# A delta-rule scan with the state's share of u taken from one matrix, formed ahead of the scan and summed in PSUM

## The chip, the cores and the metric

The kernel runs on one core of one Trainium2 chip. The metric is the device time of one execution in microseconds (us); less is better. Engines are named as in the profile: PE is TensorE's matmul (PEld its weight load), DVE is VectorE, ACT is ScalarE, POOL is GpSimd, SP is SyncE, which issues most DMAs.

## What is computed

One decoder layer for 1024 tokens and a width of 1024: a modulated RMSNorm gives h, one large projection of h feeds three token mixers (stick-breaking attention, gated DeltaNet, GLA) and their gates, and the mixers' outputs are projected, weighted, summed and projected once more. The change touches the gated DeltaNet alone. Its core in the reference, per head and per chunk:

```python
u_base, w_kc = sol[..., :dv], sol[..., dv:]
def step(state, inp):
    u_b, w_c, qk_c, qd, kd, cd = inp
    u = u_b - jnp.einsum('bhck,bhkv->bhcv', w_c, state)
    o = jnp.einsum('bhck,bhkv->bhcv', qd, state) + jnp.einsum('bhij,bhjv->bhiv', qk_c, u)
    state = state * cd[..., None, None] + jnp.einsum('bhck,bhcv->bhkv', kd, u)
    return state, o
```

`sol` solves a unit lower-triangular system for each chunk. The kernel has 4 heads and takes chunks of 128 tokens, so 8 chunks a head, in two halves of 4.

## The kernel before

**Order of the work.** PE's order is written out by the program itself; the other engines' instructions are ordered by the framework's scheduler. `emit` (L264) holds a list of tasks, each a generator that yields the time until it wants to go on, counted on a clock that adds up a fixed cost for each matmul. While no task is due, `emit` takes the next piece of the filler: `dense` (L251), the large projections. A piece is six matmuls of 512 columns into an `acc` bank (`run_cm`, L200). So PE's stream is dense work, cut by short bursts of a task. A `yield` of up to about 1300 becomes one piece of six dense matmuls.

**The DeltaNet tasks.** For each of the 8 halves (head h, half q) there are four tasks:

- `gdn_prep` (G.a, L553) transposes k into PSUM (`k_ps`), forms `Kd` (k times its decay, L585), the scalars per row (`rb`, `rn`, L593 to L596), and the triangular matrix A (L603). Then it inverts 16x16 blocks on DVE in 30 small steps (L623, L625) and sends them through DRAM.
- `gdn_inv` (G.b, L635) joins the blocks in four stages of small matmuls to Z, the transposed inverse. It starts a fixed lag after its predecessors. L649 masks the blocks on POOL; L730 writes the last quarter of Z.
- `gdn_vq` (G.v, L733) transposes v and forms `Vb` (L751), forms `qd` on POOL (L773) and `QK` (L779).
- `gdn_scan` (G.s, L781) goes through the four chunks.

**The scan of a chunk**, with S the state (128x128): a first burst computes k^T S into a bank (`s_ps`) and qd S into the output bank `o_ps`. DVE makes R = rn * (k^T S) + Vb (L797). A second burst computes Z R into `u_ps`. DVE copies it to `u` (L804). A third burst computes Kd u into `d_ps` and QK u into `o_ps`. DVE makes the new state Sn = cd * S + d_ps (L813; in a head's first chunk, which has no S, a copy, L811). Between the bursts stand the yields of 500, 1000 and 1200:

```python
s_ps = bank(pm, "mx", P)
mm(s_ps, kT[:, ts], S, 218, start=True, stop=True)
R = mid("r0", P)
nc.vector.scalar_tensor_tensor(out=R, in0=s_ps, scalar=m["rn"][:, i:i + 1],
                               in1=Vb[:, ts], op0=ALU.mult, op1=ALU.add)
mm(o_ps[:, i, :], qd[:, ts], S, 218, start=True, stop=False)
yield 500
u_ps = bank(pm, "mx", P)
mm(u_ps, Z[:, ts], R, 218, start=True, stop=True)
```

`s_ps`, `u_ps` and `d_ps` are separate tiles of the pool `pm`. All these matmuls are fp32, and each stands in the trace as two MATMUL instructions (two passes).

Of the kernel before, what the change touches and what calls it, by code (L numbers as in the profile page):

```python
# [19 lines left out]
P = 128  # L20
# [32 lines left out]
def kernel(ctx: ExitStack, tc: tile.TileContext, xT: bass.AP, c: bass.AP,  # L53
# [19 lines left out]
    def big(tag, w=1024, dt=F32):  # L73
        return mp.tile([P, w], dt, tag=tag, name=tag, bufs=3 if tag == "u5" else 2)

    def mid(tag, w=512, dt=F32):
        return sp.tile([P, w], dt, tag=tag, name=tag, bufs=1 if tag in ONE_MID else 3 if tag in ("c0", "c8", "c9") else 2)
# [225 lines left out]
    def v3(ap, c=4):  # L303
        return ap.rearrange("p (c t) -> p c t", c=c)

    def colb(ap, n, w):
        return ap.unsqueeze(2).broadcast_to([P, n, w])
# [245 lines left out]
    def gdn_prep(st, q):  # L553
        h = st["h"]
        hs = slice(q * HALF, (q + 1) * HALF)
        cs = slice(4 * q, 4 * q + 4)
        qT, kT, vT = (t[:, hs] for t in st["qkv"])
        m = st[q] = {}
        if q == 0:
            st["A"] = big("u7")  # L560
        A = st["A"][:, hs]
        gb = mid("v5")
        nc.sync.dma_start(out=gb, in_=gam_d[h:h + 1, hs].broadcast_to([P, HALF]))
        gl = v3(gb)[:, :, P - 1]
        cd = m["cd"] = mid("c0", 4)
        nc.scalar.activation(out=cd, in_=gl, func=AF.Exp)
        kdc = mid("c1", 4)
        nc.vector.tensor_sub(out=kdc, in0=gl, in1=gam_c[:, cs, h])
        nc.scalar.activation(out=kdc, in_=kdc, func=AF.Exp)
        Kd = m["Kd"] = big("u5")[:, 0:HALF]  # L570
        ss = mid("c2", 4)
        nc.gpsimd.memset(ss, 0.0)
        rr = mid("c3", 4)
        rb = m["rb"] = mid("c8", 4)
        rn = m["rn"] = mid("c9", 4)
        sq = mid("v0")
        yield from tr_free()
        tr_hold(2500)
        k_ps = bank(pt, "tr", 4, P)
        for i in range(4):  # L580
            pe_t(k_ps[:, i, :], kT[:, i * P:(i + 1) * P])
        for i in range(4):
            nc.scalar.activation(out=sq[:, i * P:(i + 1) * P], in_=k_ps[:, i, :], func=AF.Square,
                                 accum_out=ss[:, i:i + 1])
        nc.vector.tensor_tensor(out=v3(Kd), in0=k_ps, in1=colb(kdc, 4, P), op=ALU.mult)  # L585
        rstd_cols(rr, ss, 4, 1.0)
        es = mid("v0")
        nc.vector.tensor_tensor(out=v3(es), in0=K("strict").unsqueeze(1).broadcast_to([P, 4, P]),
                                in1=v3(gb), op=ALU.subtract)
        for i in range(4):  # L590
            nc.scalar.activation(out=es[:, i * P:(i + 1) * P], in_=es[:, i * P:(i + 1) * P],
                                 func=AF.Exp, bias=gam_c[:, 4 * q + i, h:h + 1])
        nc.vector.tensor_mul(out=rb, in0=rr, in1=beta_c[:, cs, h])  # L593
        nc.vector.tensor_mul(out=rn, in0=rr, in1=rr)
        nc.vector.tensor_mul(out=rr, in0=rr, in1=rb)
        nc.vector.tensor_mul(out=rn, in0=rn, in1=ncoef_c[:, cs, h])  # L596
        yield 700
        g_ps = bank(pl, "lv", 4, P)
        for i in range(4):
            ts = slice(i * P, (i + 1) * P)  # L600
            mm(g_ps[:, i, :], kT[:, ts], kT[:, ts], 218, start=True, stop=True)
        for i in range(4):
            nc.vector.scalar_tensor_tensor(out=A[:, i * P:(i + 1) * P], in0=g_ps[:, i, :],  # L603
                                           scalar=rr[:, i:i + 1], in1=es[:, i * P:(i + 1) * P],
                                           op0=ALU.mult, op1=ALU.mult)
        A3 = v3(A)
        ad = dp.tile([4, 8 * 2064], F32, tag="ad", name="ad", bufs=2)
        nc.sync.dma_start(out=ad[:, 0:P * P].rearrange("c (i t) -> i c t", t=P), in_=A3)
        L = mid("w0", 256)
        nc.sync.dma_start(  # L610
            out=L[0:32, :].rearrange("p (r x) -> p r x", x=16),
            in_=ad.rearrange("c (b x) -> (c b) x", b=8)[:, 0:2048]
                  .rearrange("n (r x) -> n r x", x=P)[:, :, 0:16])
        L3 = L[0:32, :].rearrange("p (r x) -> p r x", x=16)
        Xl = mid("w6", 256)
        nc.gpsimd.memset(Xl[0:32, :], 0.0)
        nc.gpsimd.memset(Xl[0:32, 0:256:17], 1.0)
        Xl3 = Xl[0:32, :].rearrange("p (r x) -> p r x", x=16)
        for j in range(15):
            n, w = 15 - j, j + 1  # L620
            tmp = mid("w5", 64)
            t3 = tmp[0:32, 0:n * w].rearrange("p (r x) -> p r x", x=w)
            nc.vector.tensor_tensor(out=t3, in0=L3[:, w:16, j:w].broadcast_to([32, n, w]),  # L623
                                    in1=Xl3[:, j:w, 0:w].broadcast_to([32, n, w]), op=ALU.mult)
            nc.vector.tensor_sub(out=Xl3[:, w:16, 0:w], in0=Xl3[:, w:16, 0:w], in1=t3)  # L625
        Zl = mid("w0", 256)
        nc.vector.tensor_copy(out=Zl[0:32, :].rearrange("p (r x) -> p r x", x=16),
                              in_=Xl[0:32, :].rearrange("p (r x) -> p x r", x=16))
        m["lanes"] = []
        for src in (Xl, Zl):  # L630
            xd = dp.tile([32, 256], F32, tag="xd", name="xd", bufs=4)
            nc.sync.dma_start(out=xd, in_=src[0:32, :])
            m["lanes"].append(xd)

    def gdn_inv(st, q):  # L635
# [90 lines left out]
        for ch in range(4):  # L726
# [2 lines left out]
               tile_position=(0, 0))  # L729
        nc.vector.tensor_scalar(out=Z3[0:64, :, 64:128], in0=v3(z_ps[0:64, :]),  # L730
                                scalar1=-1.0, scalar2=None, op0=ALU.mult)

    def gdn_vq(st, q):  # L733
        h = st["h"]
# [46 lines left out]
    def gdn_scan(st, q):  # L781
        h = st["h"]
        m = st[q]
        Kd, Vb, qd, QK, Z = (m[n] for n in ("Kd", "Vb", "qd", "QK", "Z"))
        kT = st["qkv"][1][:, q * HALF:(q + 1) * HALF]
        S = st.get("S")
        o_ps = bank(pm, "mx", 4, P)
        for i in range(4):
            ts = slice(i * P, (i + 1) * P)
            ch = 4 * q + i  # L790
            if S is None:
                R = Vb[:, ts]
            else:
                s_ps = bank(pm, "mx", P)
                mm(s_ps, kT[:, ts], S, 218, start=True, stop=True)
                R = mid("r0", P)
                nc.vector.scalar_tensor_tensor(out=R, in0=s_ps, scalar=m["rn"][:, i:i + 1],  # L797
                                               in1=Vb[:, ts], op0=ALU.mult, op1=ALU.add)
                mm(o_ps[:, i, :], qd[:, ts], S, 218, start=True, stop=False)
                yield 500  # L800
            u_ps = bank(pm, "mx", P)
            mm(u_ps, Z[:, ts], R, 218, start=True, stop=True)
            u = mid("r1", P)
            nc.vector.tensor_copy(out=u, in_=u_ps)  # L804
            yield 1000
            if ch < CH - 1:
                d_ps = bank(pm, "mx", P)
                mm(d_ps, Kd[:, ts], u, 218, start=True, stop=True)
                Sn = mid("r2", P)
                if S is None:  # L810
                    nc.vector.tensor_copy(out=Sn, in_=d_ps)  # L811
                else:
                    nc.vector.scalar_tensor_tensor(out=Sn, in0=S, scalar=m["cd"][:, i:i + 1],  # L813
                                                   in1=d_ps, op0=ALU.mult, op1=ALU.add)
                st["S"] = Sn
            mm(o_ps[:, i, :], QK[:, ts], u, 218, start=S is None, stop=True)
            S = st.get("S")
            if i < 3:
                yield 1200
        o = mid("v4")  # L820
        nc.vector.tensor_tensor(out=v3(o), in0=o_ps, in1=colb(m["rr"], 4, P), op=ALU.mult)
        norm_rows(o, 4, P)
        yield 5650
        yield from tr_free()
        tr_hold(2400)
        ps = bank(pt, "tr", 4, P)
        for i in range(4):
            pe_t(ps[:, i, :], o[:, i * P:(i + 1) * P])
        y = mid("v3")
        sl = slice(q * HALF, (q + 1) * HALF)  # L830
        nc.vector.scalar_tensor_tensor(out=y, in0=ps.rearrange("p c t -> p (c t)"),
                                       scalar=C("gdn_onorm"), in1=st["z"][:, sl],
                                       op0=ALU.mult, op1=ALU.mult)
        nc.sync.dma_start(out=y_dram[4 + h][:, sl], in_=y)
# [779 lines left out]
```

## Time and profile before

| | us |
|---|---|
| median of 3 runs | 1485.38 |
| lowest and highest run | 1483.48, 1486.11 |
| the profiled execution | 1483.78 |
| its span in the trace | 1482.0 |
| PE busy / DVE busy / ACT busy / POOL busy | 1441.9 / 918.8 / 697.9 / 151.5 |

The span is what the profile's rows cover; the execution's own time is 1.8 us longer. The page gives busy time by engine, a picture of the span in 40 slices, the chain of waits that ended last, and groups of instructions with the idle time of the engine just before them. Matmuls overlap in a pipeline, so the spacing of their starts says more on PE's pace than their durations.

### The profile page before, as it was taken

What the parts mean: (1) busy time and instruction counts of PE and PEld (TensorE: products, weight loads), DVE (VectorE), ACT (ScalarE), POOL (GpSimd) and SP (SyncE); (2) the same over time, 40 slices, a digit from 0 to 9 for tenths busy, and PEclk for the clock granted to TensorE, in tenths of its full rate; (3) what the DMA queues carried; (4) which work ended last, traced back from release to release, by engine and by line L of the source; (5) the groups of instructions that cost most, each with busy time, mean ns of one, the idle gap of its engine ahead of it and who ended that gap; (6) DMA issues with size and microseconds to landing.
All of it is one profiled execution on the core that took longest, in us unless ns stands there. A gap on an engine that the chain in (4) does not pass through costs nothing.

```text
span 1482.0 us, 26690 instructions
## 1 busy us (share of the span) xinstructions
PE 1441.9 (97%) x10480; PEld 1206.6 (81%) x10480; DVE 918.8 (62%) x1914; ACT 697.9 (47%) x1470; POOL 151.5 (10%) x296
## 2 busy tenths in 40 slices
PE   7999999989999999999999999999999999999998
PEld 4877777877778887979788999899988888878777
DVE  7978647476643756667666535665566326589874
ACT  5367654453733747566486524342444434342321
POOL 1032232132321000000000100010000000000000
PEclk9999999999999999999999999999999999999999
DMA  9624332131321112121212132314223425474351
GB/s 351 183 78 118 102 88 62 44 92 42 104 86 40 41 51 66 35 60 35 73 47 54 55 107 72 100 43 147 60 86 108 142 85 171 139 244 129 119 175 61
DMA packets 174567, 144.31 MB, mean 97 GB/s; under 512 B 24773, under 2 KB 140613, under 8 KB 174442
## 3 DMA queue, kind: packets, MB, share of 16 engines
q1 hardware_dynamic: 174298, 142.30, 32.3%
q8 instruction: 82, 1.34, 0.4%
q14 instruction: 43, 0.35, 0.1%
q10 hardware_dynamic: 144, 0.31, 0.1%
HBM read 110.28 MB, written 32.29 MB: 96 GB/s over the span
## 4 chain that ended last, share of the span: by engine, by line
PE 76%; DVE 12%; DMA 4%; ACT 3%; POOL 2%; issue 2%; SPq 0%; DVEq 0%; POOLq 0%; ACTq 0%
PE acc L95 62%; PE lv L95 5%; PE mx L95 5%; PE tr L122 2%; DVE w L158 2%; DVE w L625 1%; DVE ada L374 1%; DVE w L623 1%; DVE u L435 1%; DMA v<-gam_d 1%; POOL c L301 1%; POOL u L505 1%; DVE u L403 1%; DVE h_lo L408 0%; ACT w L157 0%
## 5 line engine op out<-in xcount | busy, mean ns | idle before, releaser
L95 PE MATMUL acc<-h_hi,w 128*128 128x512 f32 x1856 | 653.4, 407 | 2.4 <-ACT u L295 2.0
L95 PEld LDWEIGHTS acc<-h_hi,w 128*128 128x128 f32 x1856 | 350.3, 189 | 73.8 <-ACT u L295 2.8
L95 PE MATMUL acc<-h_lo,w 128*128 128x512 f32 x928 | 364.1, 392 | 3.0 <-DVE h_lo L408 3.0
L157 ACT CAST w<-raw 128x512 fp32r<-128x512 f32 x232 | 141.8, 620 | 220.3 <-PE acc L95 192.0
L158 DVE TENSOR_TENSOR w<-raw,w 128x512 fp32r<-128x512 f32 x232 | 158.6, 691 | 129.4 <-ACT w L157 126.8
L95 PE MATMUL acc<-w,h_hi 128*128 128x256 f32 x1280 | 238.8, 287 | 0.0
L95 PEld LDWEIGHTS acc<-h_lo,w 128*128 128x128 f32 x928 | 175.9, 190 | 29.9 <-DVE h_lo L408 3.3
L95 PEld LDWEIGHTS acc<-w,h_hi 128*128 128x128 f32 x1280 | 198.8, 191 | 1.5 <-issue 0.7
L95 PE MATMUL acc<-w,h_lo 128*128 128x256 f32 x640 | 180.8, 282 | 0.0
L95 PE MATMUL acc<-u,w 128*128 128x512 f32 x744 | 180.0, 394 | 0.5 <-DVE v L1420 0.5
L95 PEld LDWEIGHTS acc<-u,w 128*128 128x128 f32 x744 | 139.5, 188 | 33.1 <-DVE v L1420 0.9
L95 PEld LDWEIGHTS acc<-w,h_lo 128*128 128x128 f32 x640 | 122.2, 191 | 0.0
L301 POOL TENSOR_TENSOR c<-c,mhalf 128x4 f32<-128x4 f32 (+1 forms) x56 | 54.9, 981 | 600.1 <-DVE c L299 575.7
L95 PE MATMUL acc<-unit,w 128*128 128x512 f32 x312 | 79.8, 393 | 1.1 <-DVE v L1475 1.1
L1224 ACT ACTIVATE v<-acc,col 128x512 f32<-128x512 f32 x48 | 33.0, 687 | 83.9 <-PE acc L95 83.4
L95 PEld LDWEIGHTS acc<-unit,w 128*128 128x128 f32 x312 | 58.4, 188 | 14.8 <-DVE v L1475 1.5
L1167 DVE TENSOR_TENSOR_SCAN u<-u,zero_c 128x128 f32<-128x128 f32 (+7 forms) x32 | 43.4, 1357 | 35.4 <-ACT u L1165 35.4
L95 PEld LDWEIGHTS mx<-r,u 128*128 128x128 f32 x288 | 44.2, 190 | 19.2 <-DVE r L804 5.2
L95 PE MATMUL mx<-r,u 128*128 128x128 f32 x288 | 48.3, 280 | 7.7 <-DVE r L804 2.8
L95 PE MATMUL lv<-u,u 128*32 128x32 f32 (+5 forms) x528 | 48.7, 250 | 2.2 <-DVE u L706 2.1
L95 PEld LDWEIGHTS lv<-u,u 128*32 128x32 f32 (+2 forms) x528 | 40.1, 145 | 11.2 <-issue 6.7
L295 ACT COPY u<-acc 128x512 f32<-128x512 f32 x50 | 29.1, 582 | 40.2 <-PE acc L95 39.6
(273 smaller groups left out, 1984.6 us busy)
## 6 DMA issues: line engine op xcount, KB each, us to landing
raw<-in_w_in SPq DMA_DIRECT2D x160, 256.0 KB, 3.1
g_dram<-v SPq DMA_DIRECT2D x48, 256.0 KB, 2.1
v<-g_dram SPq DMA_DIRECT2D x48, 256.0 KB, 2.9
ada<-in_adaT SPq DMA_DIRECT2D x16, 512.0 KB, 8.7
u<-in_xT SPq DMA_DIRECT2D x8, 512.0 KB, 7.6
u<-in_adaT SPq DMA_DIRECT2D x8, 512.0 KB, 3.7
v<-gam_d SPq DMA_DIRECT2D x16, 256.0 KB, 3.3
y_dram<-v SPq DMA_DIRECT2D x16, 256.0 KB, 2.1
```

Of the source, the lines that this page charges most:

```text
L95: return nc.tensor.matmul(out, lhsT=lhsT, rhs=rhs, **kw)
L122: nc.tensor.transpose(out=out, in_=in_, identity=ident[:k, :k])
L157: nc.scalar.copy(out=hi, in_=raw)
L158: nc.vector.tensor_sub(out=lo, in0=raw, in1=hi.bitcast(F32))
L295: nc.scalar.copy(out=dst[:, sl], in_=ps)
L301: nc.gpsimd.tensor_tensor(out=out, in0=out, in1=mhalf[:, 0:n], op=ALU.pow)
L374: nc.vector.tensor_tensor_reduce(out=t, in0=t, in1=c_row, scale=1.0, scalar=0.0, op0=ALU.mult, op1=ALU.add, accum_out=mod[:, j:j + 1])
L403: nc.vector.scalar_tensor_tensor(out=xs[k][:, sl], in0=xs[k][:, sl], scalar=amp[:, k:k + 1], in1=rstd[:, sl], op0=ALU.mult, op1=ALU.mult)
L435: nc.vector.scalar_tensor_tensor(out=t, in0=r[:, tap:tap + T], scalar=C("conv", j + tap), in1=t, op0=ALU.mult, op1=ALU.add)
L505: nc.gpsimd.tensor_scalar(out=gt[0][DA, sl], in0=raw[DA, :], scalar1=C("dt_bias")[DA, :], scalar2=None, op0=ALU.add)
L1167: nc.vector.tensor_tensor_scan(om[:, 0:n][:, ::-1], om[:, 0:n][:, ::-1], zero_c.broadcast_to([P, n]), 1.0, ALU.mult, ALU.add)
L1224: nc.scalar.activation(out=g, in_=ps, func=AF.Identity, bias=C("merge_b", gi * 8 + d))
```

## The change

- `gdn_prep` keeps a second product of `k_ps`: ACT copies it to `Kt` (the upper half of the u5 tile whose lower half is Kd), and DVE multiplies it by `rn` per row.
- `gdn_inv` gets one more step at its end: after a yield of 650, four matmuls of Kt^T and Z form MT = (Z^T diag(rn) k)^T per chunk in an `lv` bank, and ACT copies that over `Kt`.
- `gdn_scan` takes one PSUM bank, `w_ps`, for the whole half, with two slots for u and two for d in turn. u is now summed in PSUM: Z Vb (`from_v`), and on top of it MT S. R and its DVE instruction are gone, and a chunk has two bursts: MT S and qd S; then Kd u, QK u and the next chunk's `from_v`.

```diff
@@ gdn_prep
-        Kd = m["Kd"] = big("u5")[:, 0:HALF]
+        kk = big("u5")
+        Kd, Kt = kk[:, 0:HALF], kk[:, HALF:]
+        m.update(Kd=Kd, MT=Kt)
...
         nc.vector.tensor_tensor(out=v3(Kd), in0=k_ps, in1=colb(kdc, 4, P), op=ALU.mult)
+        nc.scalar.copy(out=v3(Kt), in_=k_ps)
...
         nc.vector.tensor_mul(out=rn, in0=rn, in1=ncoef_c[:, cs, h])
+        nc.vector.tensor_tensor(out=v3(Kt), in0=v3(Kt), in1=colb(rn, 4, P), op=ALU.mult)
@@ gdn_inv
+        yield 650
+
+        MT = m["MT"]
+        m_ps = bank(pl, "lv", 4, P)
+        for i in range(4):
+            ts = slice(i * P, (i + 1) * P)
+            mm(m_ps[:, i, :], MT[:, ts], Z[:, ts], 218, start=True, stop=True)
+        nc.scalar.copy(out=v3(MT), in_=m_ps)
@@ gdn_scan
-        o_ps = bank(pm, "mx", 4, P)
+        o_ps, w_ps = (bank(pm, "mx", 4, P) for _ in range(2))
+
+        def from_v(i):
+            ts = slice(i * P, (i + 1) * P)
+            first = q == i == 0
+            mm(w_ps[:, i % 2, :], Z[:, ts], Vb[:, ts], 218, start=True, stop=first)
+
+        from_v(0)
         for i in range(4):
             ts = slice(i * P, (i + 1) * P)
             ch = 4 * q + i
-            if S is None:
-                R = Vb[:, ts]
-            else:
-                s_ps = bank(pm, "mx", P)
-                mm(s_ps, kT[:, ts], S, 218, start=True, stop=True)
-                R = mid("r0", P)
-                nc.vector.scalar_tensor_tensor(out=R, in0=s_ps, scalar=m["rn"][:, i:i + 1],
-                                               in1=Vb[:, ts], op0=ALU.mult, op1=ALU.add)
+            u_ps, d_ps = w_ps[:, i % 2, :], w_ps[:, 2 + i % 2, :]
+            if S is not None:
+                mm(u_ps, MT[:, ts], S, 218, start=False, stop=True)
                 mm(o_ps[:, i, :], qd[:, ts], S, 218, start=True, stop=False)
-                yield 500
-            u_ps = bank(pm, "mx", P)
-            mm(u_ps, Z[:, ts], R, 218, start=True, stop=True)
             u = mid("r1", P)
             nc.vector.tensor_copy(out=u, in_=u_ps)
             yield 1000
             if ch < CH - 1:
-                d_ps = bank(pm, "mx", P)
                 mm(d_ps, Kd[:, ts], u, 218, start=True, stop=True)
...
             if i < 3:
+                from_v(i + 1)
                 yield 1200
```

**PE, the first chunk of a scan that has a state (head 0, second half).** The names: r2 is S, r0 is R, r1 is u, u2 is k^T, u5 is Kd (after the change the same tile also holds MT), u8 holds Z and QK, u6 holds Vb and qd. A "waits" note gives the counter that the instruction waits for and so the engine, not the instruction. Each line of "..." stands for the rest of six dense matmuls. Before:

```order
L95 MATMUL mx_2218<-r2_1861,u2_537 128x128
L95 MATMUL mx_2217<-r2_1861,u6_2091 128x128 [waits Pool_49]
...
L95 MATMUL mx_2235<-r0_2220,u8_1976 128x128 [waits DVE_49]
...
L95 MATMUL mx_2258<-r1_2237,u5_1145 128x128 [waits DVE_49]
L95 MATMUL mx_2217<-r1_2237,u8_1976 128x128
...
L95 MATMUL mx_2269<-r2_2260,u2_537 128x128 [waits DVE_49]
L95 MATMUL mx_2217<-r2_2260,u6_2091 128x128
```

And with the change:

```order
L95 MATMUL mx_2253<-u6_2175,u8_1986 128x128 [waits DVE_49]
L95 MATMUL mx_2253<-r2_1845,u5_1147 128x128 [waits Activation_49]
L95 MATMUL mx_2252<-r2_1845,u6_2175 128x128 [waits Pool_49]
...
L95 MATMUL mx_2253<-r1_2257,u5_1147 128x128 [waits DVE_49]
L95 MATMUL mx_2252<-r1_2257,u8_1986 128x128
L95 MATMUL mx_2253<-u6_2175,u8_1986 128x128 [waits DVE_49]
...
L95 MATMUL mx_2253<-r2_2266,u5_1147 128x128
L95 MATMUL mx_2252<-r2_2266,u6_2175 128x128
```

The burst with r0 and its six dense matmuls are gone. The burst with u has a third matmul, Vb by Z for the next chunk, with a DVE wait of its own. The first matmul with the new state (r2_2266) has no wait.

**PE, the end of the inverse (same half).** w7 and w6 belong to the inverse's last stage, cst by u3 is the transpose of v. Before:

```order
L95 MATMUL lv_2085<-w7_2039,w6_2023 64x64 [waits DVE_49,Activation_49,Pool_49]
L95 MATMUL lv_2085<-w7_2039,w6_2023 64x64 x3
L122 MATMUL lv_2097<-cst_106,u3_546 128x128 [waits PE_49]
L122 MATMUL lv_2097<-cst_106,u3_546 128x128 x3
L95 MATMUL lv_2103<-u2_1115 128x128 [waits PE_49]
```

And with the change:

```order
L95 MATMUL lv_2157<-w7_2148,w6_2063 64x64 [waits DVE_49,Activation_49,Pool_49]
L95 MATMUL lv_2157<-w7_2148,w6_2063 64x64 x3
L95 MATMUL acc_2150<-h_hi_297,w_1782 128x512
...
L95 MATMUL lv_2169<-u8_1986,u5_1147 128x128 [waits DVE_49]
L95 MATMUL lv_2169<-u8_1986,u5_1147 128x128 x3
L122 MATMUL lv_2181<-cst_106,u3_546 128x128 [waits PE_49]
```

Six dense matmuls and the four that form MT have come between the inverse's last stage and v's transposes; MT's burst waits for DVE's last write of Z.

**DVE, around two chunks of that scan.** L623 and L625 (L627 and L629 with the change) are the small steps of another half's block inverse. Before:

```order
L625 TENSOR_TENSOR w6_2116<-w6_2116,w5_2161 32x15 [waits DVE_49]
L766 TENSOR_TENSOR v1_2980<-cst_106,v5_2953 128x512 [waits DMAHW7_49,Pool_49]
L627 COPY w0_2164<-w6_2116 32x256 [waits DVE_49]
L797 SCALAR_TENSOR_TENSOR r0_2305<-mx_2303,c9_1150,u6_2091 128x128 [waits PE_49]
L804 COPY r1_2316<-mx_2314 128x128 [waits PE_49]
L158 TENSOR_TENSOR w_2596<-raw_2597,w_2596 128x512 [waits DMAHW6_49,Activation_49]
L813 SCALAR_TENSOR_TENSOR r2_2326<-r2_2293,c0_1140,mx_2324 128x128 [waits PE_49]
```

And with the change:

```order
L814 COPY r1_2278<-mx_2253 128x128 [waits PE_49]
L629 TENSOR_TENSOR w6_2089<-w6_2089,w5_2131 32x2x14 [waits DVE_49]
L627 TENSOR_TENSOR w5_2134<-w0_2087,w6_2089 32x15 [waits DVE_49]
L629 TENSOR_TENSOR w6_2089<-w6_2089,w5_2134 32x15 [waits DVE_49]
L631 COPY w0_2137<-w6_2089 32x256 [waits DVE_49]
L822 SCALAR_TENSOR_TENSOR r2_2288<-r2_2266,c0_1142,mx_2253 128x128 [waits PE_49]
L568 TENSOR_TENSOR c1_2903<-v5_2899,gam_c_683 128x4 [waits DMAHW7_49]
L814 COPY r1_2301<-mx_2253 128x128 [waits PE_49]
L822 SCALAR_TENSOR_TENSOR r2_2310<-r2_2288,c0_1142,mx_2253 128x128 [waits PE_49]
```

R's instruction is gone. Of a chunk the copy of u and the new state are left on DVE, with the other work of the half still between them; the copy of u and the new state now read one tile (mx_2253).

## Rows read from the trace of the kernel before

**Rows 1.** The page, part 1: busy time of each engine (share of the span), instructions.

```profile
PE 1441.9 (97%) x10480; PEld 1206.6 (81%) x10480; DVE 918.8 (62%) x1914; ACT 697.9 (47%) x1470; POOL 151.5 (10%) x296
```

**Rows 2.** Waits of PE from 120 to 490 us: total us, times, longest.

```profile
PE mx L95 <- DVE r L804: 2.8, 3, 1.5
PE lv L95 <- POOL u L456: 2.6, 1, 2.6
PE mx L95 <- POOL u L773: 2.6, 2, 2.1
PE lv L95 <- DVE u L706: 2.1, 2, 1.2
...
PE mx L95 <- DVE r L813: 1.1, 2, 0.9
PE mx L95 <- DVE r L797: 1.0, 1, 1.0
PE lv L95 <- POOL w L649: 1.0, 1, 1.0
```

**Rows 3.** Timeline, an undisturbed third burst: start, duration, engine, instruction [idle before <-releaser].

```profile
233.63 0.61 PE L95 MATMUL mx<-r,u 128*128 128x128 f32 x4
...
233.99 0.48 PE L95 MATMUL acc<-h_hi,w 128*128 128x512 f32 x1
234.05 0.35 DVE L813 SCALAR_TENSOR_TENSOR r<-r,c,mx 128x128 f32<-128x128 f32 x1 [0.16 <-PE mx L95]
...
234.31 0.39 PE L95 MATMUL acc<-h_lo,w 128*128 128x512 f32 x1
...
234.54 0.63 PE L95 MATMUL acc<-h_hi,w 128*128 128x512 f32 x2
```

**Rows 4.** Timeline, a first burst that waits for the new state.

```profile
228.44 0.33 DVE L813 SCALAR_TENSOR_TENSOR r<-r,c,mx 128x128 f32<-128x128 f32 x1
...
228.83 0.71 PE L95 MATMUL mx<-r,u 128*128 128x128 f32 x4
...
229.62 0.40 PE L95 MATMUL acc<-h_lo,w 128*128 128x512 f32 x1
```

**Rows 5.** Timeline, third bursts and their new states: first of 24, slowest, last.

```profile
180.38 0.61 PE L95 MATMUL mx<-r,u 128*128 128x128 f32 x4
180.80 0.29 DVE L811 COPY r<-mx 128x128 f32<-128x128 f32 x1 [1.32 <-PE mx L95]
...
387.95 0.61 PE L95 MATMUL mx<-r,u 128*128 128x128 f32 x4
390.47 0.33 DVE L813 SCALAR_TENSOR_TENSOR r<-r,c,mx 128x128 f32<-128x128 f32 x1
...
475.01 0.61 PE L95 MATMUL mx<-r,u 128*128 128x128 f32 x4
475.43 0.35 DVE L813 SCALAR_TENSOR_TENSOR r<-r,c,mx 128x128 f32<-128x128 f32 x1 [0.33 <-PE mx L95]
```

**Rows 6.** Line 813 in the trace: ns min/median/max; idle time of DVE before it.

```profile
L813 DVE SCALAR_TENSOR_TENSOR r<-r,c,mx x24: 325/347/349, 186.1 to 475.4; 128x128 f32<-128x128 f32 x24
...
  PE mx L95: 13.8, 14
```

**Rows 7.** Groups of instructions like the added ones: busy us, mean ns | idle before.

```profile
L585 DVE TENSOR_TENSOR u<-tr,c 128x512 f32<-128x512 f32 x8 | 5.5, 684 | 3.6 <-ACT v L583 3.6
...
L295 ACT COPY u<-acc 128x512 f32<-128x512 f32 x50 | 29.1, 582 | 40.2 <-PE acc L95 39.6
```

**Rows 8.** Timeline of POOL, the masks of the inverse that PE waits for.

```profile
325.28 2.84 POOL L649 TENSOR_SCALAR w<-w,cst 128x64 f32<-128x64 f32 x2 [1.99 <-DMA w<-xd]
```

**Rows 9.** Stretches: PE, PEld, DVE, ACT, POOL busy us, granted clock, DMA share, GB/s.

```profile
110.00:114.40 4.40, 0.56 (x3) 0.15 (x2) 4.27 (x9) 2.06 (x4) 0.10 (x1) 1.00 0.42 122
114.40:118.20 3.80, 3.79 (x12) 3.12 (x13) 3.23 (x6) 1.57 (x3) 0.00 (x0) 0.56 0.97 251
...
215.00:235.00 20.00, 16.82 (x86) 13.53 (x85) 15.04 (x49) 10.94 (x23) 3.77 (x5) 1.00 0.31 86
```

More of the change, by code (lines that the diff above doesn't have):

```diff
@@ L574, in gdn_prep @@
         rb = m["rb"] = mid("c8", 4)
-        rn = m["rn"] = mid("c9", 4)
+        rn = mid("c9", 4)
         sq = mid("v0")
@@ L783, in gdn_scan @@
         m = st[q]
-        Kd, Vb, qd, QK, Z = (m[n] for n in ("Kd", "Vb", "qd", "QK", "Z"))
-        kT = st["qkv"][1][:, q * HALF:(q + 1) * HALF]
+        Kd, Vb, qd, QK, Z, MT = (m[n] for n in ("Kd", "Vb", "qd", "QK", "Z", "MT"))
         S = st.get("S")
-        o_ps = bank(pm, "mx", 4, P)
+        o_ps, w_ps = (bank(pm, "mx", 4, P) for _ in range(2))
[4 more added lines that the diff above has]
+        from_v(0)
         for i in range(4):
```

## The prediction

> **What bounds the kernel now.** I began with busy time by engine [rows 1]: PE is busy for 97% of the span and no other engine for more than 62%. PE's order is written out, and whatever is added to it has no free engine time to fall into: a matmul more costs its own time, and a wait of PE counts in full. So I read next whom PE waited for in the stretch of the DeltaNet tasks, 120 to 490 us [rows 2]. The scans (`mx`) lose 7.5 us there in eight waits, the inverses (`lv`) most of the rest. From about 490 us on the order of PE is the same before and after, and everything before 120 us is too, so the change is worth what it does to this stretch. Last I read the timeline of single bursts, for what an undisturbed burst, a wait and the way from Kd u to the new state take [rows 3 to 5]. The reader is to see there that the dense work between two bursts hides DVE's part of a chunk completely when DVE is free: behind the third burst DVE writes the new state at 234.05 to 234.40, while PE is in the first of six dense matmuls.
>
> **The matmuls.** A half before issues, per chunk, k^T S, qd S, Z R, Kd u and QK u; after, Z Vb, MT S, qd S, Kd u and QK u. That is the same number, heads' first and last chunks included. New are four matmuls for MT in each of eight halves: 32. In [rows 3] a burst of two matmuls (four passes) starts at 233.63, and the second dense matmul behind it at 234.31, where dense matmuls follow each other at 0.23: 234.31 - 0.23 - 233.63 = 0.45, so 0.22 a matmul. That is all that a burst costs; starting one has no price of its own, and having 28 bursts fewer and eight more gives nothing back. **+7.2 us** for 32 x 0.22.
>
> **The wait that moves.** This is the large term. In the order with the change, `from_v` of the next chunk is the third matmul of the burst Kd u, QK u, and has a wait for DVE. The burst's first matmul has by then waited for u. The MT S that reads the new state, one piece later, has no wait left. So the wait in between must be the one for the new state: `from_v` writes a slot of the same tile `w_ps` from which DVE still reads d. Before, that wait stood in front of the next first burst, behind six dense matmuls. Now only QK u stands between Kd u and it. It occurs after chunks 0, 1 and 2 of each half: 24 times.
>
> Its price, from [rows 3]: the burst starts at 233.63, and its two matmuls would let a third begin at 234.08. DVE's new state ends at 234.40. PE goes on 0.06 after DVE's end, which is 228.44 + 0.33 = 228.77 against PE at 228.83 in [rows 4]: 234.46, so 0.38 late. A burst that had to wait also starts up more slowly: from 228.83 to the second dense matmul behind it it took 0.79, so 0.56 without the dense spacing, against 0.45: 0.11 more. Together 0.49 where DVE is free, and **11.8 us** for 24. That is the low end.
>
> DVE isn't always free. It took up the new state straight from idleness in 14 of 24 cases of L813 [rows 6]. Reading all 24 chunks in question in this way (first, slowest and last are in [rows 5]), a matmul in `from_v`'s place would have been 0.32 to 0.51 late in 17 of them, and 0.69 to 2.46 in seven, 17.9 in all; with 24 x 0.11 that is 20.5 us, the high end. What makes the seven late are the small steps of another half's block inverse and the scalars of `gdn_prep`, which stand in front of the new state in DVE's order; with the change such work still stands there (the third place shown), in eight of 24 chunks, in somewhat smaller sums. I take 5.0 for the lateness beyond the quick case, nearer to its high end of 8.7 than to nothing: **+16.8 us**.
>
> **What goes.** Each wait in [rows 2] costs about 0.28 more than its row says: the dense matmul ahead of it is shown busy for 0.39 or 0.40 at a spacing of 0.23, and 0.11 is the slow start. The wait for R (L797) goes with R: 1.0 + 0.28 = 1.3. Those for the new state in front of the first burst (L813) are paid in the new place: 1.1 + 2 x 0.28 = 1.7. A matmul more (qd S) now lies between the one that makes u and the one that needs it, and one more (Z Vb) ahead of qd S at a scan's start: 0.22 less for each of three waits for u and two for qd, 1.1. **-4.1 us**. A few waits too short for [rows 2] would add up to one more; I leave them to the range.
>
> **DVE, ACT, POOL and the queues.** DVE loses 28 instructions of about the size of L813 and gains eight of 128x512 like L585; ACT gains 16 copies like L295 [rows 7]. Both sit in the cover of dense matmuls. Where they do not: the copy and the product lengthen the way to A by up to 0.6 + 0.7, and so the way to the block inverse, on which the masks of the inverse wait. PE lost 2.6 + 1.0 to these masks (the 2.6 goes under a POOL instruction that ended last; the masks run until 328.1 [rows 8]). The order of the tasks shifts by several dense pieces there, in either direction. These two waits may vanish (-4.2 with their 0.28 each) or stay. MT's burst is a new wait for DVE's last write of Z behind one piece of cover; the like wait for L706 was late in two of eight halves, 2.1 + 2 x 0.28 = 2.7, so this one costs between nothing and 2.7. ACT's copy of MT has three pieces of dense matmuls until its reader. No DMA is added. In SP's order the loads of the masks' inputs change places by one or two with loads of weights, in both directions; PE waited for no weights in [rows 2], so what this moves is again the masks. For all of this I take **-1.0 us**, between -4.2 and +2.7.
>
> **The sum.** 1483.8 (the profiled execution's own time) + 7.2 + 16.8 - 4.1 - 1.0 = 1502.7. The median of the runs is 1.6 above the profiled execution, the short waits left out are worth about -1: I say **1502 us**. The low ends give 1483.8 + 7.2 + 11.8 - 5.1 - 4.2 = 1493.5, the high ends 1483.8 + 7.2 + 20.5 - 4.1 + 2.7 = 1510.1.
>
> [...] That the wait is for the new state I read from the order and from a shared tile; u's slot and d's slot don't overlap. [...] No run shown here tells what would happen without the wait.
>
> **Rivals.**
>
> *The wait costs nothing* (the change doesn't put it there, or the counter has always been reached): 1483.8 + 7.2 - 4.1 - 1.0 = 1485.9, no change. Against it: the shortest way in [rows 5] is from 180.38 to 181.09, and the burst's two matmuls cover 0.45 of it. 5%.
>
> *Faster: the slack that the new form gives.* If all eight waits of the scans vanish (7.5 + 8 x 0.28 = 9.7), and the masks' two (4.2), and the wait for the new state is free: 1483.8 + 7.2 - 9.7 - 4.2 = 1477.1. It decides on the 24 waits: with these gains, faster by over 0.2% needs them under (9.7 + 4.2 - 7.2 - 3.0) / 24 = 0.15 us each, where [rows 3, 4] say 0.49. 4%.
>
> *DVE late each time.* If at every new state one more 128x512 instruction (0.68, [rows 7]) is still running: 24 x (0.49 + 0.68) = 28.1, and 1514. For it: the slow cases of [rows 5]; against it: 14 of 24 from idleness [rows 6]. 7%.
>
> *The clock.* [...] 3%. [...]
>
> **How the numbers follow.** 81% for the forecast with its own ends of 1493.5 to 1510.1, 5% for no change, 4% for faster, 7% and 3% for the two above. The range goes a little past the ends, since the lateness on DVE depends on an order that is new throughout: 1492 to 1512. About 0.2%, 3 us, is what a measurement of this kernel can tell from no change. Faster 4%, the same 6%, slower 90%.
>
> **What would show it.** Right: in the profile after, PE waits in `mx` for L822 some 24 times, 0.3 us and more each, inside the burst between QK u and the dense work; the waits for L797 are gone; the stretch of the DeltaNet tasks is about 18 us longer and what follows is not. The MATMUL instructions number 64 more, two for each of 32. Wrong: few or no waits for L822 (then the first rival), a granted clock under 1.00 in the scans (the last), or a difference behind the DeltaNet tasks.

## The result, and the profile after

| | before | after |
|---|---|---|
| median of 4 runs | 1485.46 us | 1502.92 us |
| lowest and highest | 1483.48, 1486.11 | 1501.65, 1505.29 |
| the profiled execution | 1483.78 | 1503.27 |
| its span | 1482.0 | 1501.5 |

The ratio is 1.0121, with a 95% interval of 1.0107 to 1.0135: slower by 17.5 us. The forecast was 1502.

Busy time of the engines in the changed kernel, part 1 of its page, answers to [rows 1]:

```profile
PE 1455.2 (97%) x10544; PEld 1217.1 (81%) x10544; DVE 914.0 (61%) x1894; ACT 706.9 (47%) x1487; POOL 156.3 (10%) x296
```

64 matmul instructions more, as foretold. PE is busy 13.3 us longer in a span 19.5 longer, so waiting has grown too. The waits of PE in the stretch of the DeltaNet tasks (total us, times, longest) answer to [rows 2]:

```profile
PE mx L95 <- DVE r L822: 8.6, 20, 1.2
PE lv L95 <- DVE u L710: 3.6, 1, 3.6
PE mx L95 <- POOL u L785: 1.7, 2, 1.6
PE lv L95 <- ACT w L675: 1.2, 1, 1.2
PE tr L122 <- DVE v L857: 1.0, 1, 1.0
PE lv L95 <- DVE w L680: 1.0, 2, 0.7
PE lv L95 <- DVE u L734: 0.9, 1, 0.9
PE mx L95 <- DVE r L814: 0.7, 2, 0.4
PE mx L95 <- DVE r L820: 0.6, 4, 0.2
```

L822 and L820 write the new state (L820 behind a head's first chunk): 24 waits that were not there before. The wait for R is gone, and so are those for the masks. L814 is the copy of u, L785 qd's product on POOL, L710 and L734 are writes of Z, L675 and L680 earlier steps of the stages that join the blocks. One short wait, from the timeline of PE and DVE, to be held against [rows 3]:

```profile
193.32 0.61 PE L95 MATMUL mx<-r,u 128*128 128x128 f32 x4
193.74 0.35 DVE L822 SCALAR_TENSOR_TENSOR r<-r,c,mx 128x128 f32<-128x128 f32 x1
194.15 0.49 PE L95 MATMUL mx<-u,u 128*128 128x128 f32 x2 [0.22 <-DVE r L822]
194.39 0.48 PE L95 MATMUL acc<-h_hi,w 128*128 128x512 f32 x1
194.70 0.39 PE L95 MATMUL acc<-h_lo,w 128*128 128x512 f32 x1
```

The burst starts at 193.32, and `from_v` could start 0.45 later, at 193.77. It starts at 194.15, 0.06 behind the end of the new state: 0.38 late. The bracket says 0.22, since the matmuls ahead are shown busy for 0.61, where `from_v` could have started 0.45 behind their start. From 194.15 to the second dense matmul are 0.55, where one matmul (0.22) and the dense spacing (0.23) would take 0.45: 0.10 of slow restart. A late one, where DVE is in another half's block inverse (L627, L629):

```profile
231.59 0.71 PE L95 MATMUL mx<-r,u 128*128 128x128 f32 x4 [0.34 <-DVE r L814]
...
232.93 0.21 DVE L627 TENSOR_TENSOR w<-w,w 32x63 f32<-32x63 f32 x1
233.07 0.33 DVE L822 SCALAR_TENSOR_TENSOR r<-r,c,mx 128x128 f32<-128x128 f32 x1
...
233.46 0.49 PE L95 MATMUL mx<-u,u 128*128 128x128 f32 x2 [1.15 <-DVE r L822]
```

I took the same reading of every matmul between 122 us and the last scan: its start against the one before, less the spacing that such matmuls have undisturbed (0.231 for 512 columns, 0.111 for a pass of 128x128). What is over, in us:

| what ended the gap | before | after |
|---|---|---|
| the new state, 24 waits in the second burst | - | 13.2 |
| other waits of the scans | 9.8 | 3.7 |
| waits of the inverses | 9.3 | 7.5 |
| waits of transposes | - | 1.7 |
| nothing; PE at its lower clock (after: 0.50 granted in 175 to 180 us) | 0.2 | 2.2 |
| gaps under 0.15 each, the slow restarts among them | 19.7 | 22.6 |
| sum | 39.0 | 50.9 |

With 64 passes x 0.111 = 7.1 the difference is 19.0. PE also reached its wait for the gates 1.3 later in this execution, before any DeltaNet task. Together that is the 20.3 by which the last scan's bursts start later. The order is the same again from the 7,172nd matmul from the end, which starts 20.6 later, at 512.17 instead of 491.60; the last one starts 19.5 later. To within the 1.1 that goes away behind the stretch, the change is worth what it does to the DeltaNet stretch, as foretold.

### The profile page after: what moved, and what is told of

The parts are those of the page before. It is cut to its first block, busy times and chain, and to the rows that moved or that the text cites. A ratio compares the mean times of both kernels' runs of the same rounds, so it can differ in the third digit from the quotient of the medians.

```text
span 1501.5 us, 26818 instructions
## 1 busy us (share of the span) xinstructions
PE 1455.2 (97%) x10544; PEld 1217.1 (81%) x10544; DVE 914.0 (61%) x1894; ACT 706.9 (47%) x1487; POOL 156.3 (10%) x296
## 4 chain that ended last, share of the span: by engine, by line
PE 77%; DVE 13%; ACT 3%; DMA 3%; POOL 2%; issue 2%; SPq 0%; POOLq 0%; DVEq 0%; ACTq 0%
PE acc L95 63%; PE lv L95 6%; PE mx L95 5%; PE tr L122 2%; DVE w L158 1%; DVE w L629 1%; DVE u L435 1%; DVE w L627 1%; DVE ada L374 1%; POOL c L301 1%; DMA v<-gam_d 1%; POOL u L505 1%; DVE h_lo L408 1%; DVE u L403 0%; ACT w L157 0%
## 5 line engine op out<-in xcount | busy, mean ns | idle before, releaser
L95 PE MATMUL lv<-u,u 128*32 128x32 f32 (+5 forms) x592 | 58.2, 255 | 4.5 <-DVE u L710 3.6
L95 PEld LDWEIGHTS lv<-u,u 128*128 128x128 f32 (+2 forms) x592 | 49.2, 152 | 13.9 <-issue 6.9
L95 PE MATMUL mx<-u,u 128*128 128x256 f32 (+1 forms) x180 | 38.1, 291 | 9.3 <-DVE r L822 8.6
L435 DVE SCALAR_TENSOR_TENSOR u<-u,col,u 128x1024 f32<-128x1024 f32 x36 | 46.0, 1285 | 0.1
```

Of the source, the lines that this page charges most:

```text
L95: return nc.tensor.matmul(out, lhsT=lhsT, rhs=rhs, **kw)
L435: nc.vector.scalar_tensor_tensor(out=t, in0=r[:, tap:tap + T], scalar=C("conv", j + tap), in1=t, op0=ALU.mult, op1=ALU.add)
```

## Experiments

Times are medians, beside runs of the kernel before on the same chip. Over the series its median went from 1483.4 to 1486.2, so I compare by the ratio; 0.1 of a per cent is 1.5 us, and most ratios are known to 0.1 to 0.2 of a per cent either way.

| | us | ratio to before | 95% interval |
|---|---|---|---|
| the change | 1502.92 | 1.0121 | 1.0107 to 1.0135 |
| d in a bank of its own | 1494.16 | 1.0063 | 1.0041 to 1.0086 |
| from_v ahead of the next burst | 1494.65 | 1.0070 | 1.0052 to 1.0089 |
| from_v sooner | 1508.75 | 1.0173 | 1.0150 to 1.0195 |
| MT formed, not used | 1495.26 | 1.0074 | 1.0054 to 1.0094 |
| copy and product only | 1491.70 | 1.0040 | 1.0027 to 1.0053 |
| matmuls at MT's place only | 1495.03 | 1.0062 | 1.0047 to 1.0077 |
| 32 matmuls, order kept | 1490.96 | 1.0034 | 1.0022 to 1.0047 |
| from_v ahead, copy and product off the way to A | 1498.57 | 1.0089 | 1.0074 to 1.0103 |
| before, later stages | 1495.76 | 1.0070 | 1.0058 to 1.0083 |
| from_v ahead, two lane buffers | 1488.48 | 1.0020 | 1.0012 to 1.0029 |
| before, two lane buffers | 1486.18 | 1.0007 | 0.9997 to 1.0017 |
| from_v ahead, off the way to A, two lane buffers | 1498.12 | 1.0082 | 1.0068 to 1.0096 |

### The wait: taken away in two ways, and made longer

The changed kernel, with d in a bank of its own:

```diff
-            u_ps, d_ps = w_ps[:, i % 2, :], w_ps[:, 2 + i % 2, :]
+            u_ps = w_ps[:, i % 2, :]
...
+                d_ps = bank(pl, "lv", P)
                 mm(d_ps, Kd[:, ts], u, 218, start=True, stop=True)
```

> The changed kernel, with Kd u written to a bank of its own (one of the three banks that the inverses use in turn) instead of the tile of u's slots. Order of PE the same. Theory A (the time goes to 24 waits of from_v for the new state, there only because u and d share a tile): the waits inside the burst go, the way from Kd u to the new state is then covered by QK u, from_v and six dense matmuls; the profile after shows 13.4 us in those waits by start spacing, and 24 x 0.10 of slow restart: 1502.9 - 15.8 = 1487, between 1484 and 1490. Rival B (DVE is the bound of the scans, and a wait taken away comes back at the next MT S): over 1498, with about as much waiting for the new state in front of the first bursts. Rival C (the extra matmuls, copies and the new order of the tasks cost nearly all of the 17.5): over 1500, few waits changed.

The changed kernel, with `from_v` at the head of the next first burst, behind the dense piece:

```diff
             if i < 3:
-                from_v(i + 1)
                 yield 1200
+                from_v(i + 1)
```

> The changed kernel, with from_v of the next chunk issued at the head of the next first burst (behind the dense piece) and no longer at the end of the second burst; u and d share their tile as before. Theory A: the wait on the new state stays in the program, but stands behind six dense matmuls (1.4 us) as the wait of the kernel before did, and costs only where DVE is late by more than that, 1 to 2 us in all: 1487 to 1489, and within 2 us of the run with a bank of its own. Rival B: over 1498. Rival C: over 1500.

And `from_v` directly behind Kd u:

```diff
+            if i < 3:
+                from_v(i + 1)
             mm(o_ps[:, i, :], QK[:, ts], u, 218, start=S is None, stop=True)
             S = st.get("S")
             if i < 3:
-                from_v(i + 1)
                 yield 1200
```

> The changed kernel, with from_v of the next chunk directly behind Kd u, ahead of QK u. One matmul less (0.22) then stands between Kd u and the wait for the new state. Theory A: each of the 24 waits is 0.22 longer, those with DVE late too: 1502.9 + 5.3 = 1508, between 1506.5 and 1510. Rival B (DVE is the bound of the scans: PE gives back what it loses) and rival C (the waits are not where the time goes): within 2 us of the changed kernel.

In the first two the waits of the second burst are gone, by two edits that have nothing in common but that. Moving d took its tile and its bank away together, so what the wait goes by, tile or bank, stays open. With `from_v` sooner, each short wait is 0.605 by starts instead of 0.38; the timeline shows two passes of Kd u, the state, and `from_v` behind it:

```profile
195.07 0.38 PE L95 MATMUL mx<-r,u 128*128 128x128 f32 x2
...
195.49 0.35 DVE L822 SCALAR_TENSOR_TENSOR r<-r,c,mx 128x128 f32<-128x128 f32 x1
...
195.90 0.49 PE L95 MATMUL mx<-u,u 128*128 128x128 f32 x2 [0.44 <-DVE r L822]
196.22 0.39 PE L95 MATMUL mx<-r,u 128*128 128x128 f32 x2
```

24 x 0.22 = 5.4 were due, and the ratio rose by 0.52 of a per cent, 7.7 us, which holds 5.4 within its uncertainty; 1508 was expected. So the mechanism is shown. The size is not: taking the waits away should have brought 15.6 (15.8 in the expectation) and brought 8.6 and 7.6. Theory A's ranges (1484 to 1490, and 1487 to 1489) were missed, and rivals B and C (over 1498 and 1500) as well.

With d in a bank of its own, 2.7 of the 15.6 comes back by starts as waits for u, 2.6 as waits of the inverses and 1.7 at the lower clock (0.59 granted in 173 to 180 us); where PE's order is the same again, that profile is 8.8 ahead of the changed kernel's. The bank given to d is one of the three that the inverses use in turn; whether sharing them costs something was not tested. With `from_v` ahead, PE's waits for u, then its waits in the last stage, 1250 to 1400 us, where the changed kernel has none:

```profile
PE lv L95 <- DVE u L710: 3.5, 3, 2.7
PE mx L95 <- DVE r L814: 2.6, 3, 1.7
```

```profile
PE acc L95 <- DVE v L1430: 1.1, 1, 1.1
PE acc L95 <- ACT v L1393: 0.9, 1, 0.9
PE acc L95 <- DVE v L1398: 0.3, 1, 0.3
```

By starts, the waits for u are 1.0 in the changed kernel and 3.4 here (3.6 before): where DVE is late, the wait for the new state had covered the wait for u behind it. That much is rival B. Up to the 7,200th matmul from the end this profile is 13.1 ahead of the changed kernel's, 1.2 of it before any DeltaNet task. Behind that point it gives back 3.2, 2.7 of it (by starts) in the last three rows; why PE waits there stays open. Of 15.6 in waits and restarts, 9.9 are left in the profiled pair.

### What forming MT costs

The kernel before, with all of MT formed and not used; with the copy and the product alone; with the matmuls alone, on Kd and Z; and with as many matmuls where they move nothing else (the clock by which the work is ordered does not count them):

```diff
...
+        nc.scalar.copy(out=v3(Kt), in_=k_ps)
...
+        nc.vector.tensor_tensor(out=v3(Kt), in0=v3(Kt), in1=colb(rn, 4, P), op=ALU.mult)
...
+        yield 650
...
+        for i in range(4):
+            ts = slice(i * P, (i + 1) * P)
+            mm(m_ps[:, i, :], MT[:, ts], Z[:, ts], 218, start=True, stop=True)
+        nc.scalar.copy(out=v3(MT), in_=m_ps)
```

> The kernel before, with everything that forms MT (the copy of k, the product with rn, the four matmuls of each half, the copy of MT) added, and MT not used: the scan is that of the kernel before, with three bursts. Theory A: 32 matmuls x 0.22 = 7.2, and the order of the tasks shifts as in the change, which may take away waits for the masks (up to 4) or add some (up to 3): 1485.5 + 7.2 - 1 = 1492, between 1488 and 1496. Rival C: forming MT is the cost, 1500 to 1505. Rival E (matmuls in a longer burst cost nothing): within 2 us of the kernel before.

> The kernel before, with only ACT's copy of k and DVE's product with rn added in gdn_prep: no matmul added, and their result not used; the scan and the order of PE are those of the kernel before. Theory A2: the wait at 169 us grows from 1.1 to 2.5 or more and the clock falls behind it, 3 to 5 us: 1484 + 4 = 1488, between 1486.5 and 1489.5. Rival F (gdn_prep is covered, only PE's order and matmuls count): within 1 us of the kernel before. With the next run it should add up to the 11.9 us that forming MT without use cost.

> The kernel before, with only the four 128x128 matmuls at the end of each half's inverse (on Kd and Z, their result is not read): no copy, no product. Theory A2: 32 x 0.22 = 7.2, and the order of the tasks shifts, which may take away waits for the masks (up to 4) or add some: 1484 + 7.2 - 1 = 1490, between 1487 and 1492. Rival F: 1494 to 1496, as with MT formed and not used, for the order alone would bring the 5 us at 169 us. Rival E (extra matmuls in a burst cost nothing): within 2 us of the kernel before.

```diff
             mm(q_ps[:, i, :], kT[:, ts], qT[:, ts], 218, start=True, stop=True)
+            mm(q_ps[:, i, :], kT[:, ts], qT[:, ts], 0, start=True, stop=True)
```

> The kernel before, with the four matmuls k^T q of each half issued twice into the same place (32 128x128 matmuls more, not counted in the clock by which the order of the work is made): the order of everything else stays as it was, no copy, no product. The second issue makes QK 0.9 us later, which the scan reads some microseconds behind. If a matmul more in a burst costs its own time and nothing else: 32 x 0.22 = 7.0, 1485 + 7 = 1492, between 1490.5 and 1493.5. Rival E (they find room in PE's waits): 1485 to 1488. Rival C (any work added shifts the waits behind it by as much again): 1495 or more, as with the matmuls on Kd and Z.

Forming MT costs 11.0, the upper end of theory A's range. The matmuls where they move nothing cost 5.0 (3.3 to 7.0), within the range expected though under the 7.0; in the profiled pair their stretch is 6.8 longer. At MT's place they cost 9.2, as rival F had it: this profile's DeltaNet stretch is 10.2 longer, 7.1 of it passes and 3.1 waits and restarts. Copy and product alone cost 5.9 (4.0 to 7.9), by the median more than both theories had, with PE's order unchanged. Theory A2 held here only in its place: the wait near 169 us (3.3 by starts, 1.1 before); the clock behind it stayed at 1.00. The parts do not add up (5.9 + 9.2 against 11.0). Some waits are lengthened by both: those for the writes of Z (L706, L710 here) are 2.5 by starts before, 3.8 and 4.6 with a part, and 4.4 with the whole.

### The wait at 169 us

PE waits there for L710 in the first half's inverse. On DVE the block inverse of the third half stands ahead, which starts when its lanes, the blocks of A laid out anew by way of DRAM, have been loaded (`w<-ad` on SP). The timelines of SP, before and after, then of POOL and DVE after:

```profile
159.81 0.80 SPq L632 DMA_DIRECT2D xd<-w  x2
162.21 0.38 SPq L647 DMA_DIRECT2D w<-xd  x1
162.68 0.46 SPq L610 DMA_DIRECT2D w<-ad  x1
```

```profile
159.90 2.20 SPq L636 DMA_DIRECT2D xd<-w  x2
164.00 0.38 SPq L651 DMA_DIRECT2D w<-xd  x1
164.46 0.46 SPq L614 DMA_DIRECT2D w<-ad  x1
```

```profile
166.73 1.28 POOL L785 TENSOR_TENSOR u<-u,v 128x512 f32<-128x512 f32 x1
...
166.97 1.06 DVE L627 TENSOR_TENSOR w<-w,w 32x15 f32<-32x15 f32 x1 [2.33 <-DMA w<-ad]
...
169.94 0.47 DVE L627 TENSOR_TENSOR w<-w,w 32x48 f32<-32x48 f32 x1
170.45 0.47 DVE L629 TENSOR_TENSOR w<-w,w 32x48 f32<-32x48 f32 x1
...
172.34 0.27 DVE L710 TENSOR_SCALAR u<-lv 32x128 f32<-32x128 f32 x1
```

The same instructions before:

```profile
150.94 1.28 POOL L773 TENSOR_TENSOR u<-u,v 128x512 f32<-128x512 f32 x1 [1.72 <-ACT v L772]
...
165.25 0.18 DVE L623 TENSOR_TENSOR w<-w,w 32x15 f32<-32x15 f32 x1 [1.18 <-DMA w<-ad]
...
168.96 0.27 DVE L706 TENSOR_SCALAR u<-lv 32x128 f32<-32x128 f32 x1
```

A is ready long before (its last instruction on DVE starts at 152.2, the load is issued at 164.5). Then DVE is slow: steps that take 0.20 elsewhere take up to 1.06 and 0.48, and L710 comes at 172.3, against 168.96 before. Of these 3.4, 1.3 are the later start of the whole stretch. Less that, the block inverse starts 0.5 later, and its 13 steps up to L710 take 5.4 instead of 3.7: in this trace the slow steps are the larger part. The first of them runs beside L785, the first of POOL's eight products for `qd`. Before, that product ran at 150.94, ahead of this block inverse; here ACT's input to it (L784) ends at 165.24, where the like L772 ended at 150.86. With the copy and the product alone it comes late as well, at 166.18.

The lanes go into the tile `w0`, of which there is one, from which the half before writes its result out. Two edits follow from this: A sooner (on top of `from_v` ahead), or two buffers for `w0`; then both, and the second alone on the kernel before.

```diff
-        nc.scalar.copy(out=v3(Kt), in_=k_ps)
         rstd_cols(rr, ss, 4, 1.0)
...
                                  func=AF.Exp, bias=gam_c[:, 4 * q + i, h:h + 1])
+        nc.scalar.copy(out=v3(Kt), in_=k_ps)
...
-        nc.vector.tensor_tensor(out=v3(Kt), in0=v3(Kt), in1=colb(rn, 4, P), op=ALU.mult)
         yield 700
...
+        nc.vector.tensor_tensor(out=v3(Kt), in0=v3(Kt), in1=colb(rn, 4, P), op=ALU.mult)
         L = mid("w0", 256)
```

> The run with from_v ahead (1494.7), and in gdn_prep ACT's copy of k moved behind the four Exp, and DVE's product with rn behind the DMA that takes A out. [...] Rival F (the place near 169 us hangs on the shifted order of the tasks, not on gdn_prep): within 1.5 us of 1494.7, with the wait and the lower clock still there.

```diff
-    ONE_MID = ("w0", "w2", "w3", "w4", "w5", "w7", "v5")
+    ONE_MID = ("w2", "w3", "w4", "w5", "w7", "v5")
```

> The run with from_v ahead (1494.7), with two buffers instead of one for the tile w0, into which a half's lanes for the block inverse are loaded and from which the half before writes its result out. Theory G: the load of the lanes (w from ad, on SP) has to wait for that one buffer, and in the traces with the copy and the product it goes out at 163 to 166 us, 14 us behind its A; the block inverse that follows on DVE stands ahead of L710, for which PE waits near 169 us. With two buffers the load goes out near 153, the wait at 169 falls to under 1 us and the lower clock behind it goes: 1494.7 - 5 = 1490, between 1487 and 1492. Rival H (DVE itself has too much to do between 145 and 175 us): the block inverse starts earlier and now stands ahead of L680 too; PE waits as long or longer there, 1494 or more.

> The kernel before, with two buffers for w0; nothing of the change in it. Theory G: the wait for L706 at 169 us (1.1 there, 2.5 in all eight halves) goes, and nothing else gets worse: 1485 - 2 = 1483, between 1480 and 1484. Rival H: a wait for L676 takes its place, 1487 or more.

> Two edits together: the copy of k and the product with rn off the way to A (alone it made the kernel slower, 1498.6), and two buffers for w0 (with from_v ahead: 1488.5). If what made the first slower was only that the lanes' load stood in SP's order behind the one buffer (issued at 165.9 with A ready at 150.9), then with two buffers it goes out before 160, the wait near 169 us is under 2.4 and the earlier A is worth something: 1486 to 1489. If the earlier copy and product displaced other work on ACT, DVE and SP by themselves: 1490 or more, with waits of 3 us or more near 228 or 399 us as in the run without the second buffer.

With two buffers the load goes out at 158.86 (162.25 with one; 153 was hoped for), and the median falls by 0.50 of a per cent, 7.4 us, to 1488.48, a time that theory G had. Its mechanism is shown in part only: the wait at 169 us falls from 2.8 by starts to 2.3, not to under 1, and the lower clock behind it stays (0.60 in 172 to 182 us). Of the 7.4, the two profiled executions show 2.0, and 0.8 in the DeltaNet stretch; the one with two buffers was the slowest of its 11. Where the rest lies these profiles do not show. For the kernel before the second buffer does nothing that can be measured, which neither theory had: the wait for L706 shrinks and one for L676 (2.0 near 164 us) takes its place, rival H's mechanism, at a lower price than it gave.

A sooner made it worse: 13.2 over before (1498.57). I had expected 1490, 1488 to 1492, from a wait for L710 of 1.2 or less and no loss of clock behind it; the rival's range was missed as well. A was ready 5.6 us behind the transposes of k instead of 7.7, at 150.9, but the load went out only at 165.93, and PE waited 5.0 at 169 us. With two buffers as well that wait falls to 2.3, and the kernel stays 12.2 over before: the second expectation there. One of the waits that keep it so, PE's for the new state, and what DVE does in the meantime, from the timeline with both edits:

```profile
399.85 0.67 DVE L590 TENSOR_TENSOR v<-cst,v 128x512 f32<-128x512 f32 x1
...
401.42 0.17 DVE L596 TENSOR_TENSOR c<-c,beta_c 128x4 f32<-128x4 f32 x1 [0.77 <-POOL c L301]
...
402.04 0.69 DVE L612 TENSOR_TENSOR u<-u,c 128x512 f32<-128x512 f32 x1
...
402.78 0.33 DVE L822 SCALAR_TENSOR_TENSOR r<-r,c,mx 128x128 f32<-128x128 f32 x1
...
403.17 0.49 PE L95 MATMUL mx<-u,u 128*128 128x128 f32 x2 [3.54 <-DVE r L822]
```

On DVE the state comes behind steps of another half's `gdn_prep`, one of which (L596) waits 0.77 for POOL, and behind the moved product: it starts at 402.78, 0.05 behind the end of L612.

### The kernel before, with more time between the stages

```diff
-        yield 1050
+        yield 1500
...
-        yield 700
+        yield 1100
...
-        yield 400
+        yield 800
...
-        yield 650
+        yield 1000
...
-        yield 800
+        yield 1000
...
-                      [f"G.v{key}"] + prev(n, 1, "G.s"), 1050))
+                      [f"G.v{key}"] + prev(n, 1, "G.s"), 2000))
```

> The kernel before, with more dense pieces between the stages of the inverse and between gdn_vq and the scan (1050 to 1500, 700 to 1100, 400 to 800, 650 to 1000, 800 to 1000, and 1050 to 2000 ahead of the scan). No instruction added or taken away; nothing of the change in it. In the profile of before PE lost 2.1 to L671, 2.5 to L706, 3.9 to the masks, 0.6 to L676 and 3.0 to the product on POOL: 12.1 us. If half of that is covered by the dense work that now stands there: 1484 - 6 = 1478, between 1474 and 1482. Rival: the waits move with DVE and POOL, which are behind for other reasons: within 2 us of the kernel before.

10.4 slower, against both expectations. By starts the waits for L671 grew from 2.1 to 6.6, those for R from 1.2 to 4.7, and PE lost 8.1 at its lower clock (0.59 granted in 166.2 to 172 us). The waits for the masks and L706 did go, and that for POOL's product fell from 3.0 to 1.0, but the others took more than that. No version here beats the kernel before; the best form with MT is 3.0 (1.8 to 4.3) behind it.

## Why the prediction was right

- **The matmuls, +7.2.** Right by the trace: in an MT burst at 222.12 eight passes take until 223.12, 1.00, less 0.10 of restart 0.22 a matmul, 7.1 for 32. By time alone the matmuls cost 5.0 (3.3 to 7.0).
- **The wait that moves, +16.8.** Right in place, number and size: 24 waits, 0.38 where DVE is free (0.32 behind a head's first chunk), 0.10 of restart, and late in eight chunks, as the order had it. They sum to 13.2 + 2.4 = 15.6; beyond the short case 4.3 where I had taken 5.0. The tag "0.3 us and more" does not hold as the profile prints it: a short wait stands there with 0.22.
- **What goes, -4.1.** The scans' other waits fell by 6.1. The waits for u went from 3.6 to 1.0, and I had taken 0.7 off: a chunk that waits for the new state finds u ready more often. That is the cover that the first two experiments lose again (3.7 and 3.4).
- **DVE, ACT, POOL and the queues, -1.0.** This is the weak step. The masks' waits vanished (-3.9, the low end), yet transposes, the lower clock and the wait for L710 more than took their place: 9.5 before, 11.4 after, +1.9, inside the bounds of -4.2 and +2.7. I had followed the longer way to A to the masks. What the change costs here is paid in front of L710, on DVE, where another half's block inverse stands ahead: it starts 0.5 later, and its slow steps add 1.7, 0.9 of it in the one that ran beside POOL's moved product. That this product would move there I had not looked at, and that the copy and the product cost 5.9 (4.0 to 7.9) by themselves I had not foreseen. MT's own new wait, for L734, was 1.1, within its bounds.
- **The sum.** 7.1 + 15.6 - 6.1 + 1.9 = 18.5 against 18.9 predicted: three terms were off by 1 to 3 us, with both signs; that they cancel to 0.4 is luck. The 1 us taken off for waits too short to list did not show: the gaps under 0.15 grew by 2.9, and the restarts are 2.4 of that. Its large term was a gross one: by the medians, undoing the wait brings only about half of it back.
- **The rivals.** DVE was late in eight chunks and not in 24, and the short waits did not lower the clock: 225 to 300 us holds six of them and has 1.00.

## What to carry to other kernels

Look for a write that the change puts into a tile from which another engine still reads. Here `from_v` wrote one slot of `w_ps` while DVE read another, and waited for DVE 24 times, 0.38 each where DVE was free; behind the dense work that already hides the reader, or with d in a tile and a bank of its own, these waits were gone. Count a wait's price gross, and expect less from taking it away: of 15.6 here 8.6 and 7.6 came back, and with `from_v` ahead the waits for u rose from 1.0 to 3.4. And in a schedule as tight as this one (PE busy for 97%) take no instruction off the bounding engine for free until you have followed what is queued behind it: the copy and the product cost 5.9 (4.0 to 7.9) with PE's order unchanged.

## What the runs showed of the hardware

**The lower clock came after some waits and not after others as long.** Stretches of a wait and of what follows (columns as in [rows 9]): in the changed kernel at 169 us, with d in its own bank at 400 us, and before at 325 us:

```profile
169.30:173.00 3.70, 0.31 (x2) 0.00 (x0) 3.46 (x13) 1.52 (x2) 2.15 (x5) 1.00 0.38 80
173.00:179.50 6.50, 6.29 (x28) 4.74 (x29) 4.70 (x21) 1.85 (x3) 0.82 (x3) 0.64 0.28 86
```

```profile
400.00:402.80 2.80, 0.97 (x5) 0.50 (x4) 2.80 (x13) 2.75 (x4) 0.00 (x0) 1.00 0.02 8
402.80:407.00 4.20, 4.20 (x17) 3.62 (x18) 3.36 (x10) 2.60 (x6) 1.49 (x1) 0.59 0.84 240
```

```profile
325.40:328.20 2.80, 0.17 (x6) 0.03 (x4) 2.80 (x5) 0.34 (x1) 2.76 (x3) 1.00 0.29 80
328.20:335.00 6.80, 6.80 (x155) 5.02 (x156) 4.90 (x19) 3.64 (x6) 1.72 (x7) 1.00 0.12 43
```

Of these three waits PE did least in the last, and only there the clock stayed at 1.00. In the first, 6.5 us at 0.64 lose 2.3 us, and the next 2.5 at 0.56 another 1.1, an estimate from the shares not granted (6.5 x 0.36, 2.5 x 0.44). With the copy and the product alone, PE waited 3.1 us at the place of the first (busy for 0.17 us of 168.9 to 172.2), and the clock stayed at 1.00 up to 180. What tells the cases apart, these runs do not say.

**Some DVE instructions ended only with POOL's product.** L627 at 166.97 took 1.06 us where the like instruction of before took 0.18, and ended at 168.03, POOL's L785 at 168.01. Beside five more of the eight L785 in this trace one DVE instruction took 1.23 to 1.32 and ended 0.02 to 0.08 behind L785 (at 233.57, 315.95, 322.29, 399.27 and 412.20). Beside the last, L820, at 445.14, took 0.29, as at its three other places. With the copy and the product alone, a step at 166.36 took 1.15 and ended 0.04 behind L777, the same product. What sets the cases apart was not tested. By the durations, an estimate, the step at 166.97 makes 0.9 (1.06 - 0.18) of the 3.8 us (by starts) that PE waited at 169.
